# Output projection of a two-layer decoder step, issued in stages over all eight output tiles

## Chip, cores and metric

The kernel runs on one core of a Trainium2 chip. TensorE (PE) multiplies, VectorE (DVE) and ScalarE (ACT) work on its results, GpSimd (POOL) does small side work, SyncE (SP) issues all DMA transfers in one queue, in program order. The metric is the device time of one execution in microseconds, lower is better.

## What is computed

Two layers, each a SwiGLU feed-forward, a token mixer and a second feed-forward. 512 prompt tokens and 8 sample tokens (each with a state of its own) go through together. Of the mixer, this matters here:

```python
p_conv, p_z, p_b, p_a, p_q, p_k, p_v = jnp.split(h @ w_in, SPLIT_POINTS, axis=-1)
dn_out, S_new, conv_new = _deltanet(p_conv, p_z, p_b, p_a, conv_buf, S0, ...)   # 4 heads, 512 columns
swa_out = _swa_banded(q, k, v, swa_sinks)       # prompt: window of 128, 8 heads, 512 columns
swa_out, k_new, v_new = _swa_step(q, k, v, k_buf, v_buf, swa_sinks)   # samples
mix = jnp.concatenate([dn_out, swa_out], axis=-1) @ w_out     # 1024 x 1024
x = x + m[:, 5] * mix
```

The delta rule runs over chunks of the prompt, one after the other through a state S; each needs the inverse of a triangular matrix. For the samples it is one step from a state S0 of 8 x 4 matrices of 128 x 128, which is written back.

## The kernel before

Activations lie transposed (features on partitions): 8 blocks k of 128 input features, and two halves of the tokens, half 0 with 256 and half 1 with 264 columns (256 prompt, 8 samples). Weights are streamed from HBM as `raw` tiles and split by ACT and DVE into a high and a low part (`whi`/`wlo`, or `khi`/`klo` where the split block is kept in a slot of its own), each for 4 blocks k; the activations are split too (`hh`, `hl`). A product is three matmuls for each block k (`mmk`, line 659): hi x hi, hi x lo, lo x hi.

Everything is recorded in one Python pass, and each engine runs its own instructions in that order. `Clock` keeps an estimate of when each engine is free, and `Fill` holds generators of small work (delta-rule inverse, merges of the blocks of the inverse, scan, window attention, sample heads), ordered by the numbers in `RANK`. `fill.step()` puts steps of that work between the large matmuls where the estimate says that they are ready; `fill.until(cond)` records such work alone until a condition holds. So the order is set by these calls, by the ranks and by the estimates.

In `mix` (line 1036) the input projection ends with the tiles z0 to z2. What is then left is small work: for head pair 0 and 1 `dn_inverse` (a chain of 21 small operations on DVE, tiles `bb`, `w`, `t`, `wt`), `dn_merge` (tiles `XT`, `X`, `mb`, `wt`), `scan` (four chunks, tiles `kd`, `R`, `vn`, `S`), `normed` (writes `hh`/`hl`, blocks 0 to 3), `swa_chain` (window attention, blocks 4 to 7), and for the samples `dn_sample`, which does one head pair after the other in `sample_pair`: it loads the states (`s<-in_s`), multiplies them by zero-padded vectors (32 small matmuls, `aux<-s,pad`), sends a row through memory and back (`vnd`, `bv`), updates and writes the states (`s<-bv,misc,s`, `out_ss`). Only after both pairs does it write the sample columns of blocks 0 to 3 in half 1 (`hh<-on`, `hl<-on`).

The output projection is a `tail` (line 770): for half 0, output tile m = 0 to 7, each over all k; then half 1 in the same way. Its function `wait` holds half 0 until all blocks of chunks 0 and 1 are there, and half 1 until those of chunks 2 and 3 and of the samples are. `KEEP = 1` tile's weights are kept for half 1, tiles 4 to 7 stay in the ring of 8 split blocks, tiles 1 to 3 are loaded and split again. Half 0 accumulates in tiles `acc` (two of two banks each, a bank for each output tile), half 1 in `aux` (four of one bank). `xupdate` (line 689) adds a finished tile to the residual x on DVE, `Norm` sums the squares for the next norm.

Of the kernel before, what the change touches and what calls it, by code (L numbers as in the profile page):

```python
# [17 lines left out]
KD = D // 128  # L18
# [7 lines left out]
SLOTS = 51  # L26
PARTS = ((0, 11), (11, 22))
FIRST = 4
KEEP = 1
RANK = {"scan": 1.2, "merge": 9.9, "inverse": 5.4, "taps": 3.5, "front": 3, "normed": 1.0, "prep": 4.3, "keep": 7.0, "dn_s": 2.3, "swa_s": 2.0, "swa": 5.2}  # L30
BACKLOG = {"act": 2.4, "dve": 7.7}
TUNE = {"spare": 5, "steps": 8}
# [270 lines left out]
class Ops:  # L303
# [17 lines left out]
    def dma(self, out, in_):  # L321
        self.nc.sync.dma_start(out=out, in_=in_)
        nbytes = 4 * out.shape[0] * self.cols(out)
        self.clk.run("dma", max(0.45, nbytes / 330e3), [out], [in_], 1.4 if nbytes < 65536 else 2.6)

    def mm(self, out, lhsT, rhs, start, stop, frac=1.0, join=False):

        self.nc.tensor.matmul(out, lhsT=lhsT, rhs=rhs, start=start, stop=stop, skip_group_check=join)  # L328
        n = self.cols(rhs)
        if rhs.dtype == F32R:  # L330
            cost = max(0.107, n / 2400)
        else:
            cost = n / 600 if n >= 128 else 0.0033 * out.shape[0]
        cost = cost * frac + 0.011 * min(frac, 1.0)
        self.clk.run("pe", cost, [out], [lhsT, rhs])
# [43 lines left out]
    def tt(self, **k):  # L379
        self._dve("tensor_tensor", self.cols(k["out"]), k)  # L380

    def stt(self, **k):
        self._dve("scalar_tensor_tensor", self.cols(k["out"]), k)
# [22 lines left out]
def trunk(ctx, tc, xT, cT, cst, rope, vec, gu1, dn1, win, wba, wout, gu2, dn2, ada,  # L406
# [13 lines left out]
    fill = Fill(clk)  # L420

    used, given = set(), [0]

    def slot(name, dt=F32, shape=(128, NT), own=False):
        t = slot_p.tile(list(shape), dt, tag="s", name=name, bufs=SLOTS)
        if not own:
            used.add(t.tensor.name)
        return t
# [11 lines left out]
    W = Stream(ops, raw_p, hl_p, 4, 8, lambda: slot("sum", F32, (128, 512)), drop)  # L440

    def room_for(n):
        return len(used) + given[0] + n <= SLOTS - spare[0]
# [3 lines left out]
    def hold(n):  # L447

        yield lambda: room_for(n)
        given[0] += n  # L450

    def acc():
        t = ps.tile([128, 2, 512], F32, tag="acc", name="acc", bufs=2)
        clk.ring("acc", 2, t)
        return t

    def aux(shape=(128, 512)):
        t = ps.tile(list(shape), F32, tag="aux", name="aux", bufs=4)
        clk.ring("aux", 4, t)
        return t  # L460

    def small(name, shape, dt=F32, bufs=1):
        return con.tile(list(shape), dt, name=name, tag=name, bufs=bufs)
# [195 lines left out]
    def mmk(out, w, k, src, kk, a, first, last, M=128, join=False):  # L659

        wh, wl = w
        for wi, (wt_, part) in enumerate(((wh, 0), (wh, 1), (wl, 0))):
            mm(out, lhsT=wt_[:, k * M:(k + 1) * M], rhs=src(a, part, kk), start=first and wi == 0, stop=last and wi == 2,
               join=join)
# [24 lines left out]
    def xupdate(l, j, m, p, a):  # L689
        o = HALF[a][0]  # L690
        assert (l, 3 * j + 2) in mod_done
        g = mt[l][:, (3 * j + 2) * 8 + m, :]
        stt(out=x[:, m, o:o + 256], in0=p[:, 0:256], scalar=g[:, 0:1], in1=x[:, m, o:o + 256],
            op0=ALU.mult, op1=ALU.add)
        if a == 1:
            t8 = small("t8", (128, NS), bufs=2)
            tt(out=t8, in0=p[:, 256:264], in1=g[:, 1:9], op=ALU.mult)
            tt(out=x[:, m, T:NT], in0=x[:, m, T:NT], in1=t8, op=ALU.add)
# [71 lines left out]
    def tail(l, j, items, nk, norm, src, last, wait=None):  # L770

        live, ws = {}, {}
        left = [sum(it[0] == a for it in items) for a in range(2)]
        for i, (a, m, fresh, more, ring) in enumerate(items):
            o, n = HALF[a]
            if wait and (i == 0 or items[i - 1][0] != a):
                wait(a)
            if a == 0:  # L780
                if i % 2 == 0:
                    ac = acc()
                p = ac[:, i % 2, 0:n]
            else:
                p = aux()[:, 0:n]
            if fresh:
                ws[m] = []
                if ring:
                    live[m] = W.out
            for k in range(nk):  # L790
                if fresh and k % 4 == 0:
                    ws[m].append(W.take(W.out - min(live.values(), default=W.out)))
                mmk(p, ws[m][k // 4], k % 4, src, k, a, k == 0, k == nk - 1)
                if ring and not more and (k % 4 == 3 or k == nk - 1):
                    live[m] += 1
                    if k == nk - 1:
                        del live[m]
                    W.advance(min(live.values(), default=W.out))
                if k % 2:
                    fill.step()  # L800
            xupdate(l, j, m, p, a)
            left[a] -= 1
            if norm is not None:
                norm.square(m, a, left[a] == 0)
            if last:
                dma(out=y_o[:, m, o:o + n], in_=x[:, m, o:o + n])
            if norm is not None and left[a] == 0:
                norm.start(a)
# [227 lines left out]
    def mix(l, norm):  # L1036
# [269 lines left out]
        ready = set()  # L1306
# [488 lines left out]
        fill.add(dn_sample(), RANK["dn_s"])  # L1795


        kept = []

        def open_keep():  # L1800
            yield from hold(4 * KEEP)
            for _ in range(2 * KEEP):
                keeps[l].left += 1
                kept.append(1)
                W.advance(W.out)
                yield ()

        fill.add(open_keep(), RANK["keep"])
        nrm = Norm(l, 2)

        def wait(a):
            want = {(n, pr) for n in (2 * a, 2 * a + 1) for pr in range(2)} | {(n, "a") for n in (2 * a, 2 * a + 1)}
            if a:
                want |= {"s", "as"}
            fill.until(lambda: want <= ready and (a or kept))

        items = [(0, m, True, not KEEP <= m < 4, m >= KEEP) for m in range(KD)]
        items += [(1, m, KEEP <= m < 4, False, m >= KEEP) for m in (4, 5, 6, 7, *range(KEEP), *range(KEEP, 4))]
        tail(l, 1, items, KD, nrm, h_src, False, wait)
        return nrm  # L1820


# [8 lines left out]
    keeps = [Keep() for _ in range(L)]  # L1831
    def ffn_weights(gu, dn, plain=3):
        for i in range(4):
            W.add(gu[i])
        for f0, f1 in PARTS:
            for f in range(max(f0, 2), f1):
                if f < plain:
                    W.add(gu[2 * f])
                    W.add(gu[2 * f + 1])
                else:  # L1840
                    W.add_pair(gu[2 * f], gu[2 * f + 1])
            for m in range(KD):
                for c0, c1 in ((f0, f0 + 8), (f0 + 8, f1)):
                    W.add(dn[m][:, c0 * 128:c1 * 128])

    for l in range(L):
        ffn_weights(gu1[l], dn1[l], 3 if l else FIRST)
        for i in range(22):
            W.add(win[l, i])
        for m in (*range(KD), *range(KEEP, 4)):  # L1850
            W.add(wout[l, m], keeps[l] if m < KEEP else None)
        ffn_weights(gu2[l], dn2[l], 3)


    with tc.manual_schedule():
# [8 lines left out]
        def load(q, j):  # L1864

            g, c = 2 * j + q // 2, 256 * (q % 2)
            t = []
            for k in range(0, KD, 2):
                t.append(slot("ada", F32, (128, 2, 256)))
                dma(out=t[-1], in_=ada[0, g, k:k + 2, :, c:c + 256].rearrange("k p c -> p k c"))  # L1870
            return t
# [19 lines left out]
        first = [[load(0, 0), load(0, 1)]]  # L1891
# [36 lines left out]
        for l in range(L):  # L1928
            room[0] = True
            fill.add(ada_gen(l), 9)  # L1930
            opening = None if l else lambda n: first_head(n, ada_late)
            norm = ffn(l, 0, norm, lambda l=l: Norm(l, 1), False, opening, 3 if l else FIRST)
            norm = mix(l, norm)
            room[0] = True
            fill.add(ada_gen(l + 1), 9)
            nxt = (lambda l=l: Norm(l + 1, 0)) if l + 1 < L else None
            norm = ffn(l, 2, norm, nxt, l == L - 1, None, 3)
# [142 lines left out]
```

## Time and profile before

| | |
|---|---|
| median of three runs (lowest, highest) | 2230.0 us (2226.77, 2231.2) |
| the profiled execution, its time | 2231.2 us |
| its span from first to last instruction | 2229.4 us |
| PE busy, mean granted TensorE clock | 96% of the span, 0.984 |
| DVE, ACT, POOL busy | 69%, 49%, 4% |
| DMA moved | 287.76 MB, mean 129 GB/s |

The profile shows one execution. "Busy" for PE counts a matmul from start to its modelled end, also at a lowered clock, so 96% is not 96% of the highest rate. The mixer comes twice, its end at about 627 to 765 us and again 1100 us later.

### The profile page before, as it was taken

How to read it: one execution, taken by the hardware profiler on the slowest of the kernel's cores; microseconds unless marked ns; L12 is line 12 of the kernel's file. 1: busy time of each engine (PE TensorE's matmuls, PEld its weight loads, DVE VectorE, ACT ScalarE, POOL GpSimd, SP SyncE). 2: the span in 40 equal slices, each digit the busy share in tenths (PEclk: the TensorE clock that was granted, in tenths of full speed). 3: DMA queues.
4: the chain of work that ended last, by engine and by line, in shares of the span. 5: the costliest groups of instructions: out<-in, count | busy, mean ns of one | idle time of the engine just before them, and what ended most of it. 6: DMA issues, size and time to landing. Idle time of an engine off the chain costs nothing.

```text
span 2229.4 us, 43763 instructions
## 1 busy us (share of the span) xinstructions
PE 2134.5 (96%) x17254; PEld 2015.0 (90%) x17254; DVE 1541.4 (69%) x3530; ACT 1091.0 (49%) x2342; POOL 80.5 (4%) x139
## 2 busy tenths in 40 slices
PE   7999999999978999999998999999999889999999
PEld 5898899998877889889998999999988779999999
DVE  5783596567767778458748947855686678865972
ACT  4462365356744445336535634644656345542651
POOL 0000000001011000000000000000010110000000
PEclk9999999999989999999999999999999899999999
DMA  8539634343223574773322332334332242333332
GB/s 287 198 123 305 225 105 145 105 89 103 68 70 105 192 249 139 272 261 107 103 95 69 106 106 91 105 98 106 94 102 64 71 137 86 98 104 93 107 108 72
DMA packets 177534, 287.76 MB, mean 129 GB/s; under 512 B 50448, under 2 KB 96176, under 8 KB 177328
## 3 DMA queue, kind: packets, MB, share of 16 engines
q1 hardware_dynamic: 177328, 284.96, 40.7%
q8 instruction: 135, 2.21, 0.4%
q14 instruction: 71, 0.58, 0.1%
HBM read 271.55 MB, written 14.41 MB: 128 GB/s over the span
## 4 chain that ended last, share of the span: by engine, by line
PE 83%; DVE 12%; ACT 3%; issue 1%; DMA 1%; SPq 0%; DVEq 0%; ACTq 0%
PE acc L328 48%; PE aux L328 34%; DVE wlo L363 2%; PE aux L338 1%; DVE s L363 1%; DVE cy L363 1%; DVE t L363 1%; DVE hl L363 1%; DVE y L363 1%; DVE sum L363 0%; DVE x L363 0%; ACT whi L355 0%; DVE w L363 0%; ACT s L355 0%; DMA bv<-vnd 0%
## 5 line engine op out<-in xcount | busy, mean ns | idle before, releaser
L355 ACT ACTIVATE whi<-raw 128x512 fp32r<-128x512 f32 (+1 forms) x597 | 361.5, 616 | 423.3 <-PE acc L328 359.7
L328 PE MATMUL acc<-hh,whi 128*128 128x256 f32 (+1 forms) x1640 | 421.6, 294 | 18.0 <-DVE x L363 9.2
L363 DVE TENSOR_TENSOR wlo<-raw,whi 128x512 fp32r<-128x512 f32 (+1 forms) x597 | 390.6, 672 | 47.5 <-ACT whi L355 46.5
L328 PE MATMUL acc<-hh,wlo 128*128 128x256 f32 (+1 forms) x1640 | 407.0, 285 | 12.0 <-DVE wlo L363 12.0
L328 PE MATMUL acc<-hl,whi 128*128 128x256 f32 (+1 forms) x1640 | 406.8, 285 | 1.6 <-DVE hl L363 1.4
L328 PE MATMUL aux<-th,whi 128*128 128x264 f32 (+1 forms) x1800 | 338.4, 285 | 2.5 <-ACT u L355 2.4
L328 PEld LDWEIGHTS acc<-hh,whi 128*128 128x128 f32 x1640 | 288.7, 191 | 42.7 <-issue 20.4
L328 PEld LDWEIGHTS acc<-hh,wlo 128*128 128x128 f32 x1640 | 288.5, 191 | 14.4 <-DVE wlo L363 14.4
L328 PEld LDWEIGHTS acc<-hl,whi 128*128 128x128 f32 x1640 | 288.2, 191 | 2.4 <-DVE hl L363 2.2
L328 PEld LDWEIGHTS aux<-th,whi 128*128 128x128 f32 x1800 | 278.5, 189 | 6.4 <-ACT u L355 2.9
L328 PE MATMUL acc<-ghi,whi 128*128 128x256 f32 (+1 forms) x1320 | 274.3, 284 | 2.7 <-DVE x L363 2.7
L328 PE MATMUL acc<-ghi,wlo 128*128 128x256 f32 (+1 forms) x1320 | 272.2, 282 | 0.0
L328 PE MATMUL acc<-glo,whi 128*128 128x256 f32 (+1 forms) x1320 | 271.8, 282 | 0.0
L328 PE MATMUL aux<-th,wlo 128*128 128x264 f32 (+1 forms) x900 | 255.4, 284 | 0.0
L363 DVE SCALAR_TENSOR_TENSOR x<-acc,mt,x 128x256 f32<-128x256 f32 x136 | 61.6, 480 | 265.2 <-PE acc L328 265.2
L355 ACT ACTIVATE whi<-sum 128x512 fp32r<-128x512 f32 x300 | 187.8, 628 | 75.6 <-PE acc L328 39.8
L328 PEld LDWEIGHTS acc<-ghi,whi 128*128 128x128 f32 x1320 | 206.9, 188 | 16.8 <-issue 16.8
L328 PEld LDWEIGHTS acc<-ghi,wlo 128*128 128x128 f32 x1320 | 207.0, 188 | 0.0
L328 PEld LDWEIGHTS acc<-glo,whi 128*128 128x128 f32 x1320 | 206.7, 188 | 0.0
L363 DVE TENSOR_TENSOR wlo<-sum,whi 128x512 fp32r<-128x512 f32 x300 | 199.8, 686 | 8.3 <-ACT whi L355 7.3
L328 PE MATMUL aux<-hh,whi 128*128 128x264 f32 x604 | 172.6, 286 | 0.0
L328 PE MATMUL aux<-hl,whi 128*128 128x264 f32 x604 | 171.9, 285 | 0.5 <-DVE hl L363 0.5
(326 smaller groups left out, 3628.8 us busy)
## 6 DMA issues: line engine op xcount, KB each, us to landing
raw<-in_gu SPq DMA_DIRECT2D x176, 512.0 KB, 3.6
ada<-in_ada SPq DMA_DIRECT2D x288, 256.0 KB, 5.6
raw<-in_dn SPq DMA_DIRECT2D x64, 512.0 KB, 3.6
raw<-in_win SPq DMA_DIRECT2D x44, 512.0 KB, 3.8
raw<-in_dn SPq DMA_DIRECT2D x64, 192.0 KB, 3.2
raw<-in_wout SPq DMA_DIRECT2D x22, 512.0 KB, 4.5
s<-in_s SPq DMA_DIRECT2D x16, 256.0 KB, 3.9
bv<-vnd SPq DMA_DIRECT2D x16, 256.0 KB, 3.9
```

The costliest lines, as they stand in the source:

```text
L328: self.nc.tensor.matmul(out, lhsT=lhsT, rhs=rhs, start=start, stop=stop, skip_group_check=join)
L338: self.nc.tensor.transpose(out, in_, ident)
L355: self.nc.scalar.activation(**k)
L363: getattr(self.nc.vector, f)(**k)
```

## The change

The output projection no longer goes tile by tile. For half 0 all eight output tiles are open at once, two in each bank of the two large `acc` tiles. First come blocks k = 4 to 7 (window attention) for all eight tiles as soon as those of chunks 0 and 1 are there, then k = 0, 1 (first head pair) for all, then k = 2, 3 (second pair). Half 1 goes tile by tile as before, k = 4 to 7 first; between these and k = 0 to 3 of the first tile it waits for the delta rule's chunks 2 and 3 and for the samples (`"s"`). Weights come as half tiles of 128 x 512: k = 4 to 7 for half 0, eight blocks through `KEEP = 4` kept pairs of slots, k = 0 to 3 once, in the ring for both halves, and k = 4 to 7 again for half 1. That is 24 loads of 256 KB and 24 splits for each layer, where 11 loads of 512 KB and 22 splits stood.

```diff
-KEEP = 1
+KEEP = 4
@@ mix
         def open_keep():
-            yield from hold(4 * KEEP)
-            for _ in range(2 * KEEP):
-                keeps[l].left += 1
-                kept.append(1)
+            for _ in range(KEEP):
+                yield from hold(2)
+                keep.left += 1
                 W.advance(W.out)
-                yield ()
-        def wait(a):
-            want = {(n, pr) for n in (2 * a, 2 * a + 1) for pr in range(2)} | {(n, "a") for n in (2 * a, 2 * a + 1)}
-            if a:
-                want |= {"s", "as"}
-            fill.until(lambda: want <= ready and (a or kept))
-        items = [(0, m, True, not KEEP <= m < 4, m >= KEEP) for m in range(KD)]
-        items += [(1, m, KEEP <= m < 4, False, m >= KEEP) for m in (4, 5, 6, 7, *range(KEEP), *range(KEEP, 4))]
-        tail(l, 1, items, KD, nrm, h_src, False, wait)
+        units = [acc(), acc()]
+        def some(m, p, w, ks, k0, n, a, first, last):
+            for k in ks:
+                mmk(p[:, 0:n], w, k - k0, h_src, k, a, first and k == ks[0], last and k == ks[-1], join=True)
+                if k % 2:
+                    fill.step()
+        def part(m):
+            return units[m // 4][:, m // 2 % 2, 256 * (m % 2):256 * (m % 2) + 256]
+        wait((0, "a"), (1, "a"))
+        for m in range(KD):
+            w = W.take()
+            some(m, part(m), w, (4, 5, 6, 7), 4, 256, 0, m % 2 == 0, False)
+            kept(w)
+        wait((0, 0), (1, 0))
+        for m in range(KD):
+            ys.append(W.take(m))
+            some(m, part(m), ys[m], (0, 1), 0, 256, 0, False, False)
+        wait((0, 1), (1, 1))
+        for m in range(KD):
+            some(m, part(m), ys[m], (2, 3), 0, 256, 0, False, True)
+            xupdate(l, 1, m, part(m), 0)
+            nrm.square(m, 0, m == KD - 1)
+        nrm.start(0)
+        wait((2, "a"), (3, "a"), "as")
+        for m in range(KD):
+            p = aux()
+            w = W.take(W.out - y0[0])
+            some(m, p, w, (4, 5, 6, 7), 4, 264, 1, True, False)
+            kept(w)
+            if m == 0:
+                wait((2, 0), (3, 0), (2, 1), (3, 1), "s")
+            some(m, p, ys[m], (0, 1, 2, 3), 0, 264, 1, False, True)
+            xupdate(l, 1, m, p[:, 0:264], 1)
+            nrm.square(m, 1, m == KD - 1)
+        nrm.start(1)
@@ weights
-        for m in (*range(KD), *range(KEEP, 4)):
-            W.add(wout[l, m], keeps[l] if m < KEEP else None)
+        for m in range(KD):
+            W.add(wout[l, m][:, 512:1024], keeps[l])
+        for m in range(KD):
+            W.add(wout[l, m][:, 0:512])
+        for m in range(KD):
+            W.add(wout[l, m][:, 512:1024], keeps[l])
```

With this the recorded order changes around the projection. Three places follow, all in layer 0.

On DVE, the end of `dn_inverse` of the second head pair (`bb`, `w`, `wt` are its tiles) and what stands behind it; the lines with + are the changed kernel's, those with - the one's before:

```order
 L363 TENSOR_TENSOR hl_75<-so,hh_74 128x4x128 x2
-L363 TENSOR_TENSOR klo<-raw,khi 128x512 x2
-L363 TENSOR_TENSOR wlo<-raw,whi 128x512 x5
+L363 TENSOR_TENSOR klo<-raw,khi 128x512
 L363 TENSOR_TENSOR XT<-XT,aux 128x512
 L363 TENSOR_TENSOR X<-X,aux 128x512
```

```order
 L363 TENSOR_REDUCE w<-t 64x8x8
 L363 COPY wt<-w 64x256
+L363 TENSOR_TENSOR klo<-raw,khi 128x512
+L363 TENSOR_TENSOR X<-X,aux 128x512
 L363 TENSOR_TENSOR XT<-XT,aux 128x512
 L363 TENSOR_TENSOR X<-X,aux 128x512
```

Seven splits stood ahead of the inverse; now the first one does, and the second (`klo` of output tile 1, whose matmuls follow on PE as the 15th of the projection) stands right behind its last operation.

On PE, what stands ahead of the first sample pair's matmuls (`cs,vp` and then `s,pad`), first before:

```order
L328 MATMUL aux<-sq,cs 128x256
L328 MATMUL aux<-swa_5807,swa_6453 128x256 x2
L328 MATMUL aux<-swa_5807,swa_6565 128x256 x2
L328 MATMUL aux<-XT,mb 128x128 x4
L328 MATMUL aux<-X,wt_8283 128x128 x4
L338 MATMUL aux<-cs,vp 64x128
```

and with the change (`acc<-hh,whi` and the two behind it end the pass over k = 0, 1; `vn` to `QK` is a step of the second pair's scan):

```order
L328 MATMUL acc<-hh_74,whi 128x256
L328 MATMUL acc<-hl_75,whi 128x256
L328 MATMUL acc<-hh_74,wlo 128x256
L328 MATMUL aux<-swa_5807,swa_5799 128x256 x2
L328 MATMUL aux<-swa_5807,swa_5803 128x256 x2
L328 MATMUL aux<-vn,kd 128x128 x2
L328 MATMUL aux<-cy,S 128x128
L328 MATMUL aux<-QK,vn 128x128
L328 MATMUL aux<-cy,S 128x128
L328 MATMUL aux<-QK,vn 128x128
L338 MATMUL aux<-cs,vp 64x128
```

144 matmuls of the projection (k = 4 to 7 and k = 0, 1 of half 0) and the first two chunks of the second scan now stand ahead of the first sample pair; before, none of the projection did. Between the first and the second pair stand 36 projection matmuls, between the second pair and half 1's first matmul with `whi` 24.

On DVE, the end of the sample chain (`s<-bv,misc,s` are the state updates, `hh_76<-on` and `hl_77<-on` what half 1's blocks 0 to 3 wait for), first before:

```order
L363 SCALAR_TENSOR_TENSOR s_8544<-bv,misc,s_8544 128x128 x4
L363 SCALAR_TENSOR_TENSOR x<-acc,mt_80,x 128x256
L363 TENSOR_TENSOR ss<-ss,sq 128x256
L363 SCALAR_TENSOR_TENSOR s_8545<-bv,misc,s_8545 128x128 x4
L363 CAST hh_76<-on 128x4x8
L363 TENSOR_TENSOR hl_77<-on,hh_76 128x4x8
L363 SCALAR_TENSOR_TENSOR x<-acc,mt_80,x 128x256
```

and with the change (`ht`, `hl_75` are half 0's next norm):

```order
L363 SCALAR_TENSOR_TENSOR ht<-x,mt_80,rs 128x256
L363 SCALAR_TENSOR_TENSOR hl_75<-ht,mt_80,hh_74 128x256 x2
L363 SCALAR_TENSOR_TENSOR s_8802<-bv,misc,s_8802 128x128 x4
L363 SCALAR_TENSOR_TENSOR s_8803<-bv,misc,s_8803 128x128 x4
L363 CAST hh_76<-on 128x4x8
L363 TENSOR_TENSOR hl_77<-on,hh_76 128x4x8
L363 SCALAR_TENSOR_TENSOR x<-aux,mt_80,x 128x256
```

Before, half 0's last two updates of x stand behind `hh_76<-on`; now all of half 0, its next norm included, stands ahead of it.

## Rows read from the trace of the kernel before

**Rows 1.** The page: span, busy time of PE.

```profile
span 2229.4 us, 43763 instructions
PE 2134.5 (96%) x17254; PEld 2015.0 (90%) x17254; DVE 1541.4 (69%) x3530; ACT 1091.0 (49%) x2342; POOL 80.5 (4%) x139
```

**Rows 2.** Busy time in stretches: start to end, length, then as the first row says.

```profile
core 0: us, PE busy (x) PEld busy (x) DVE busy (x) ACT busy (x) POOL busy (x), PEclk, DMA share, GB/s
627.50:655.00 27.50, 17.55 (x102) 16.20 (x101) 17.16 (x42) 9.26 (x21) 5.19 (x4) 0.76 0.36 101
640.00:655.00 15.00, 10.52 (x44) 9.74 (x45) 6.70 (x12) 2.51 (x6) 5.19 (x4) 0.56 0.33 79
655.00:682.60 27.60, 26.68 (x213) 24.23 (x211) 20.39 (x65) 11.68 (x29) 3.86 (x5) 0.99 0.14 44
1727.00:1754.50 27.50, 17.52 (x101) 16.16 (x101) 17.19 (x42) 9.05 (x20) 5.19 (x4) 0.75 0.35 101
```

**Rows 3.** Timeline of PE: start, length, tiles, idle before; landmarks of the projection.

```profile
682.61 3.69 PE L328 MATMUL aux<-s,pad 128*32 128x128 f32 x64
...
704.99 0.37 PE L328 MATMUL acc<-hh,khi 128*128 128x256 f32 x1
...
715.02 3.69 PE L328 MATMUL aux<-s,pad 128*32 128x128 f32 x64
...
741.53 0.29 PE L328 MATMUL aux<-hh,whi 128*128 128x264 f32 x1
...
765.23 0.28 PE L328 MATMUL acc<-hh,whi 128*128 128x256 f32 x1
```

**Rows 4.** Timeline of DVE: end of the sample chain, then half 0's norm.

```profile
734.83 1.14 DVE L363 SCALAR_TENSOR_TENSOR s<-bv,misc,s 128x128 f32<-128x128 f32 x4 [2.68 <-DMA bv<-vnd]
...
737.66 0.18 DVE L363 CAST hh<-on 128x32 fp32r<-128x32 f32 x1
737.87 0.19 DVE L363 TENSOR_TENSOR hl<-on,hh 128x32 fp32r<-128x32 f32 x1
...
745.31 0.88 DVE L363 SCALAR_TENSOR_TENSOR ht<-x,mt,rs 128x256 f32<-128x256 f32 x2 [1.49 <-ACT rs L355]
```

**Rows 5.** The chain that ended last: start, length, what.

```profile
687.87 3.92 ACT s L355 x16
...
730.87 3.87 DMA bv<-vnd
```

**Rows 6.** Timeline of PE from 627 us.

```profile
627.49 1.16 PE L328 MATMUL aux<-XT,mb 128*128 128x128 f32 x8
628.48 1.06 PE L328 MATMUL aux<-wt,X 128*128 128x128 f32 x8
...
643.28 2.05 PE L328 MATMUL aux<-XT,mb 128*128 128x128 f32 x8 [5.30 <-DVE XT L363]
```

**Rows 7.** Timeline of DVE at the inverse.

```profile
630.21 3.09 DVE L363 TENSOR_TENSOR wlo<-raw,whi 128x512 fp32r<-128x512 f32 x5
...
634.41 0.28 DVE L363 TENSOR_SCALAR bb<-bb 64x256 f32<-64x256 f32 x1
...
642.17 0.37 DVE L363 COPY wt<-w 64x256 f32<-64x256 f32 x1
```

**Rows 8.** Timeline of PE: the next wait, and where full speed is back.

```profile
775.74 0.58 PE L328 MATMUL acc<-hh,wlo 128*128 128x256 f32 x1 [2.96 <-DVE wlo L363]
776.12 0.41 PE L328 MATMUL acc<-hh,whi 128*128 128x256 f32 x1
...
781.67 0.31 PE L328 MATMUL acc<-hh,wlo 128*128 128x256 f32 x1
```

**Rows 9.** Timeline of PE: two steps of the scan.

```profile
663.46 0.61 PE L328 MATMUL aux<-S,cy 128*128 128x128 f32 x4
663.90 1.06 PE L328 MATMUL aux<-wt,X 128*128 128x128 f32 x8
```

**Rows 10.** Waits of PE from 600 to 790 us: total, times, longest.

```profile
PE acc L328 <- DVE x L363: 4.7, 4, 1.6
```

More of the change, by code (lines that the diff above doesn't have):

```diff
@@ L1795, in mix @@
         fill.add(dn_sample(), RANK["dn_s"])
-        kept = []
+        keep = keeps[l]
         def open_keep():
-            yield from hold(4 * KEEP)
-            for _ in range(2 * KEEP):
-                keeps[l].left += 1
-                kept.append(1)
+            for _ in range(KEEP):
+                yield from hold(2)
+                keep.left += 1
                 W.advance(W.out)
-                yield ()
         fill.add(open_keep(), RANK["keep"])
         nrm = Norm(l, 2)
-        def wait(a):
-            want = {(n, pr) for n in (2 * a, 2 * a + 1) for pr in range(2)} | {(n, "a") for n in (2 * a, 2 * a + 1)}
-            if a:
-                want |= {"s", "as"}
-            fill.until(lambda: want <= ready and (a or kept))
@@ L1817, in mix, with wait @@
-        items = [(0, m, True, not KEEP <= m < 4, m >= KEEP) for m in range(KD)]
-        items += [(1, m, KEEP <= m < 4, False, m >= KEEP) for m in (4, 5, 6, 7, *range(KEEP), *range(KEEP, 4))]
-        tail(l, 1, items, KD, nrm, h_src, False, wait)
+        units = [acc(), acc()]
+        y0 = [0]
+        def wait(*want):
+            fill.until(lambda: set(want) <= ready)
+        def some(m, p, w, ks, k0, n, a, first, last):
[3 more added lines that the diff above has]
+                    fill.step()
@@ new lines, in kept @@
+        def kept(w):
+            keep.left += 1
+            W.advance(W.out if not y0[0] else y0[0])
+        def part(m):
+            return units[m // 4][:, m // 2 % 2, 256 * (m % 2):256 * (m % 2) + 256]
+        wait((0, "a"), (1, "a"))
+        fill.until(lambda: len(W.todo) > W.out or keep.left > 0)
+        for m in range(KD):
+            w = W.take()
+            some(m, part(m), w, (4, 5, 6, 7), 4, 256, 0, m % 2 == 0, False)
+            kept(w)
+        y0[0] = W.out
+        wait((0, 0), (1, 0))
@@ new lines, in mix @@
+        ys = []
+        for m in range(KD):
[16 more added lines that the diff above has]
+            some(m, p, ys[m], (0, 1, 2, 3), 0, 264, 1, False, True)
+            y0[0] += 1
+            W.advance(y0[0])
+            xupdate(l, 1, m, p[:, 0:264], 1)
+            nrm.square(m, 1, m == KD - 1)
@@ L1820, in mix @@
+        nrm.start(1)
+        given[0] = 0
         return nrm
```

## The prediction

> **What bounds the kernel now.** I read the page first. PE is busy 96% of a span of 2229.4 us [rows 1]; the profiled execution took 2231.2 us, so 1.8 us lie outside the span, and the three timed runs have a median of 2230.0, 1.2 us lower. A change that leaves PE's work as it is can only move PE's idle time and the time at a lowered clock. The projection has the same 384 matmuls of 256 or 264 columns in a layer before and after (8 tiles x 8 k x 3 x 2 halves), so I looked for idle time around it, in stretches.
>
> Between 627.5 us (the input projection is done, small work alone is left) and 655 us PE is busy 17.55 of 27.5 us, and the granted clock is 0.76; from 640 on it is 0.56, so nearly all of the 10.52 us that PE is busy there ran at the lower of the two levels. From 655 on PE is full again [rows 2]. Waste in this stretch: 9.95 us idle and half of 10.52, 5.3 us, together **15.3 us**. Layer 1 shows the same 1100 us later (17.52 us, 0.75 [rows 2]), so everything below counts twice.
>
> The landmarks on PE tell what the rest waits for [rows 3]. The samples' first head pair runs its matmuls at 682.61, the second at 715.02, the projection starts at 704.99, half 1 at 741.53, and at 765.23 the next sub-layer's first matmul ends the stage. Half 1 takes 765.23 - 741.53 = 23.7 us for 192 matmuls, 0.12 us each with the norm's one between. Half 1 needs `hh<-on`/`hl<-on`, which end at 737.87 + 0.19 = 738.06 [rows 4]: only 3.5 us before half 1 starts. From the first pair's matmuls to there it is 738.06 - 682.61 = **55.4 us**, a chain through two rounds of loads, small vector work and memory and back; the chain that ended last runs over it too (the wait for `bv`, 3.87 us, and the window attention's exponentials, 3.92 us, which stand ahead of it on ACT [rows 5]). So before, half 0 of the projection is the work that covers this chain, and it covers it with 3.5 us to spare.
>
> **The change, step by step, for one layer.**
>
> *More work ahead of the chain.* In the changed order 144 projection matmuls stand ahead of the first sample pair, 17.3 us at 0.12. So do the first steps of the second scan: 16 matmuls of 128 columns at 0.22 (the step from 663.46 to 663.90 holds two [rows 9]) and 4 transposes at half of that, 4.0 us; four matmuls of window attention go behind it, at the same rate about 1 us. If nothing of this fell into idle time, the chain would start 20.3 us later, at 702.9.
>
> *What falls into idle time.* The 15.3 us of waste at 627.5 to 655 are what the early matmuls could fill. They hardly do. At 627.49 the changed PE has 1.8 us of merge work (two groups of 0.9 [rows 6]) and 14 projection matmuls, 1.7 us, and is done at 631.0. The 15th needs the second `klo`, and that stands on DVE behind the whole inverse. Behind PE's waiting matmul then stand the merges of the first head pair, and behind them the scan. The inverse starts at 634.41 before; six splits of 0.6 us that stood ahead of it are gone (five take 3.09 [rows 7]), a split of activations (0.6) and four small operations that stood inside it (0.5 together, an estimate) move ahead: 634.4 - 3.7 + 1.1 = 631.8. It took 642.17 + 0.37 - 634.41 = 8.1 us [rows 7], 7.6 without those four; with the split of 0.7 PE goes on at 640.1, after 9.1 us idle. Before it went on at 643.28 after the 5.30 us wait, with waits before that [rows 6]. After a wait the clock falls: after 2.96 us it stayed at the lower level from 775.74 to 781.67, 6.0 us of matmuls 0.21 apart [rows 8]. At 0.12 the 28 matmuls of it would take 3.3, so 2.7 us are lost there; before, with sparser work, 5.3. I add 1.5 us for the next kept splits, which stand behind X and XT on DVE. Waste after: 9.1 + 2.7 + 1.5 = 13.3, so **2.0 us** are filled. The bounds are 0 and all of it, 15.3; I take 2.0, since the order on DVE decides it. The chain starts at 702.9 - 2.0 = 700.9.
>
> *The chain itself.* It takes 55.4 us before. The exponentials (3.92) stand behind the samples' operations on ACT now: -3.9. Half 0's next norm stands between its last updates, eleven vector operations of 0.4 (two take 0.88 [rows 4]), 4.4 us, of which 2.7 fall into the wait for `bv` that was there [rows 4]: +1.7. So 53.2 us. The bounds are 48.8 (the `bv` wait stays filled at no cost, 55.4 - 3.9 - 2.7) and 57.1 (55.4 + 1.7). While it runs, PE has only what is left: the third pass of half 0 and one block of half 1 (60 matmuls, 7.2 us), two times 3.7 us of sample matmuls, the last two steps of the scans and one block of window attention. Well under 53 us: PE will wait for loads of the second pair, and again for `hh<-on`.
>
> *The end.* `hl<-on` is done at 700.9 + 53.2 = 754.1. Then 180 matmuls of half 1 remain (the first tile's k = 4 to 7 are done), 21.8 us, and after a long wait the clock costs 2.7 us as above (bounds 0 and 5.3). The stage ends at 754.1 + 0.1 + 21.8 + 2.7 = 778.7, before 765.2: **13.5 us later**, 27 us for both layers.
>
> *The rest at nothing.* Two splits more on ACT and DVE, about 0.6 us each [rows 7], lie beside 34 us of idle ACT and 17 of idle DVE in the 55 us from 627.5 to 682.6 [rows 2]. 24 loads of 256 KB move 0.5 MB more than 11 of 512 KB, into a DMA share of 0.14 [rows 2]. The loads of the states now stand behind the weights' in SP's queue, and the last weight load ahead of them waits for a split that stands three operations behind the state S on DVE, 1.5 us; PE has the second scan's step to do meanwhile; without that cover it would be 1.5 us on the chain. With them at nothing the sum is 2231.2 + 27 = 2258; the median stands 1.2 lower: **2257 us**.
>
> **A rule against the layout of the banks.** Before, PE waits four times for updates of x, 4.7 us in all, because an `acc` tile is still being read [rows 10]. In the third pass four blocks in a row write one `acc` tile, each behind an update of the one before: six such waits, at 4.7/4 = 1.2 us about 7 us. I set them at nothing, since they lie in time in which PE waits for the chain anyhow. The Trainium skill (Perfetto Trace Analysis, section Matmuls) says that independent groups should rotate through different PSUM banks, so that the evacuation of one overlaps the next; here two groups share a bank and four a tile. If the waits were all on the path, the sum would be 14 us higher.
>
> **Rivals.**
>
> *The fill works, and it gets faster.* If the second split came early enough, all 15.3 us would be filled: the chain starts at 687.6, and with its lower bound `hl<-on` is done at 736.4; 0.1 + 21.8 + 2.7 later, at 761.0, the stage ends, 4.2 us early: 2231.2 - 8.4 - 1.2, about 2222. It decides from `hl<-on` at 740.6 on; each us there is 2 us of the whole. For it speaks the idle time of rows 2; against it the split's place behind the inverse. The Trainium skill (Perfetto Trace Analysis, section Optimization Strategy) says that interleaving regimes with different limits may improve performance; that is this rival, and the trace agrees that there is idle time to fill, not that it can be reached.
>
> *It cancels.* All of the waste filled and the chain at 53.2: `hl<-on` at 740.8, no change. So also if half is filled and the chain loses some further wait.
>
> *Worse than the sum.* Nothing filled (702.9), the chain at 57.1 and half of the six waits for x ahead of the second pair's matmuls (3.5): `hl<-on` at 763.5, the clock at its upper bound: 763.6 + 21.8 + 5.3 = 790.7, 25.5 us late, 2281. The updates of x stand among `s<-bv` on DVE, which speaks for it; that PE has time speaks against it.
>
> **How the numbers follow.** The measurement of this kernel tells 0.2%, 4.5 us, from no change. The sum, between about 2236 and 2272: 0.68. Worse: 0.15. Cancelled: 0.08. Faster: 0.09. So faster 0.09, same 0.08, slower 0.83. To leave out no more than 2 in 10, the range begins at 2231, in the middle of the cancelled case, and ends at 2279, near the worse one. The sum's own range, 2236 to 2272, stands beside it.
>
> **What would show it.** Right: PE idle for 8 to 10 us from about 631, ended by `klo`; the first `s,pad` at 697 to 704 instead of 682.6; then two waits on PE, one of some us ahead of the second `s,pad` (a load), one of over 10 us ahead of half 1's first `hh,whi`, ended by DVE's `hl<-on`; a fall of the clock behind each; the next sub-layer's first matmul at 774 to 783. Wrong: the first `s,pad` before 690; or `hl<-on` less than 48 us behind it; or no wait on it at all.

## The result, and the profile after

The changed kernel takes 2260.1 us (median of 4 runs, 2258.95 to 2261.74), the one before 2228.4 in the same comparison: ratio 1.0146, 95% interval [1.0131, 1.0161], slower. The forecast was 2257 us.

The page and the stretches of the changed kernel that answer to [rows 1, 2] (same columns):

```profile
span 2258.3 us, 43833 instructions
PE 2133.3 (94%) x17254; PEld 2015.3 (89%) x17254; DVE 1547.7 (69%) x3534; ACT 1094.3 (48%) x2346; POOL 80.0 (4%) x139
```

```profile
core 0: us, PE busy (x) PEld busy (x) DVE busy (x) ACT busy (x) POOL busy (x), PEclk, DMA share, GB/s
627.50:655.00 27.50, 16.30 (x120) 15.39 (x119) 15.54 (x36) 7.78 (x17) 5.13 (x4) 0.81 0.33 91
740.00:760.00 20.00, 8.34 (x37) 7.59 (x38) 15.00 (x46) 7.47 (x18) 0.73 (x9) 0.61 0.42 119
```

PE's busy time is nearly the same (2133.3 us, before 2134.5); its idle time grew. The gap at 627.5 was hardly filled (16.30 us busy for 120 matmuls, before 17.55 for 102, part of them at the lower clock), and a new one opened at 740 to 760, with 11.66 us idle.

PE's timeline of the changed kernel, the landmarks of [rows 3] and the waits between them (start, length, tiles, idle before and what ended it):

```profile
631.49 0.28 PE L328 MATMUL acc<-hl,khi 128*128 128x256 f32 x1
641.82 0.58 PE L328 MATMUL acc<-hh,klo 128*128 128x256 f32 x1 [10.05 <-DVE klo L363]
...
645.83 0.37 PE L328 MATMUL acc<-hh,khi 128*128 128x256 f32 x1
...
699.21 3.69 PE L328 MATMUL aux<-s,pad 128*32 128x128 f32 x64
...
715.49 0.39 PE L328 MATMUL acc<-hh,whi 128*128 128x256 f32 x1 [2.57 <-DVE x L363]
721.37 0.58 PE L328 MATMUL acc<-hh,whi 128*128 128x256 f32 x1 [3.57 <-DVE x L363]
...
733.52 3.69 PE L328 MATMUL aux<-s,pad 128*32 128x128 f32 x64
...
756.38 0.59 PE L328 MATMUL aux<-hh,whi 128*128 128x264 f32 x1 [11.31 <-DVE hh L363]
...
761.61 0.28 PE L328 MATMUL aux<-hh,klo 128*128 128x264 f32 x1
...
780.74 0.28 PE L328 MATMUL acc<-hh,whi 128*128 128x256 f32 x1
```

The first sample pair comes 16.6 us later than before (682.61), the second 18.5 us (715.02), the stage ends 15.5 us later (765.23). Layer 1 repeats it: the first pair at 1812.05 and the second at 1846.32, the stage's end at 1893.46 (before 1781.81, 1814.18 and 1864.28; layer 0's loss is in these too), the wait on `hh` again 11.30 us. So layer 1 lost 13.7 us of the 29.2 at its end. Behind the wait at 756.38 the matmuls stand 0.22 us apart up to 761.61, then 0.12: the lower of the two clock levels again.

DVE's timeline at the inverse and at the end of the sample chain, which answers to [rows 4, 7]:

```profile
633.34 0.27 DVE L363 TENSOR_SCALAR bb<-bb 64x256 f32<-64x256 f32 x1
...
640.80 0.37 DVE L363 COPY wt<-w 64x256 f32<-64x256 f32 x1
641.09 0.68 DVE L363 TENSOR_TENSOR klo<-raw,khi 128x512 fp32r<-128x512 f32 x1
...
747.98 1.13 DVE L363 SCALAR_TENSOR_TENSOR s<-bv,misc,s 128x128 f32<-128x128 f32 x4
749.03 0.48 DVE L363 SCALAR_TENSOR_TENSOR hl<-ht,mt,hh 128x256 fp32r<-128x256 f32 x1
...
753.65 0.48 DVE L363 SCALAR_TENSOR_TENSOR hl<-ht,mt,hh 128x256 fp32r<-128x256 f32 x1 [0.18 <-ACT hh L355]
754.06 2.18 DVE L363 SCALAR_TENSOR_TENSOR s<-bv,misc,s 128x128 f32<-128x128 f32 x8
756.16 0.17 DVE L363 CAST hh<-on 128x32 fp32r<-128x32 f32 x1
756.36 0.19 DVE L363 TENSOR_TENSOR hl<-on,hh 128x32 fp32r<-128x32 f32 x1
```

The second `klo` stands right behind the inverse's last `wt`. At the end, half 0's norm (`ht`, `hl`) fills DVE from 749 to 754 ahead of the last two state updates.

Waits of PE from 600 to 800 us (total, times, longest), which answer to [rows 10]:

```profile
PE aux L328 <- DVE hh L363: 11.3, 1, 11.3
PE acc L328 <- DVE klo L363: 11.2, 2, 10.1
PE acc L328 <- DVE x L363: 9.7, 4, 3.6
PE acc L328 <- DVE wlo L363: 4.4, 2, 2.7
```

Three waits are new or larger than before: on the samples, on `klo` and on x (before 4.7); the one on `wlo` is not. The experiments take them one by one, then together.

### The profile page after: what moved, and what is told of

It reads as the page before. It is cut to its first block, busy times and chain, and to the rows that moved or that the text cites. A ratio compares the mean times of both kernels' runs of the same rounds, so it can differ in the third digit from the quotient of the medians.

```text
span 2258.3 us, 43833 instructions
## 1 busy us (share of the span) xinstructions
PE 2133.3 (94%) x17254; PEld 2015.3 (89%) x17254; DVE 1547.7 (69%) x3534; ACT 1094.3 (48%) x2346; POOL 80.0 (4%) x139
## 4 chain that ended last, share of the span: by engine, by line
PE 82%; DVE 12%; ACT 2%; issue 1%; DMA 1%; SPq 0%; DVEq 0%; ACTq 0%
PE acc L328 48%; PE aux L328 34%; DVE wlo L363 2%; DVE s L363 1%; PE aux L338 1%; DVE hl L363 1%; DVE cy L363 1%; DVE t L363 1%; DVE ht L363 1%; DVE y L363 1%; DVE sum L363 0%; DMA raw<-in_wout 0%; ACT hh L355 0%; DVE w L363 0%; DVE x L363 0%
## 5 line engine op out<-in xcount | busy, mean ns | idle before, releaser
L355 ACT ACTIVATE whi<-raw 128x512 fp32r<-128x512 f32 (+1 forms) x573 | 347.9, 617 | 427.3 <-PE acc L328 351.4
L328 PE MATMUL acc<-hh,whi 128*128 128x256 f32 (+1 forms) x1592 | 409.8, 295 | 28.2 <-DVE x L363 19.4
L363 DVE TENSOR_TENSOR wlo<-raw,whi 128x512 fp32r<-128x512 f32 (+1 forms) x573 | 375.0, 671 | 50.6 <-ACT whi L355 50.0
L328 PE MATMUL acc<-hh,wlo 128*128 128x256 f32 (+1 forms) x1592 | 394.0, 285 | 11.5 <-DVE wlo L363 11.5
L328 PE MATMUL acc<-hl,whi 128*128 128x256 f32 (+1 forms) x1592 | 393.9, 285 | 1.9 <-DVE hl L363 1.8
L328 PEld LDWEIGHTS acc<-hh,whi 128*128 128x128 f32 x1592 | 279.8, 191 | 53.9 <-DVE x L363 21.0
L328 PEld LDWEIGHTS acc<-hh,wlo 128*128 128x128 f32 x1592 | 279.3, 191 | 14.0 <-DVE wlo L363 14.0
L328 PEld LDWEIGHTS acc<-hl,whi 128*128 128x128 f32 x1592 | 279.1, 191 | 3.2 <-DVE hl L363 2.9
L328 PE MATMUL aux<-hh,whi 128*128 128x264 f32 x556 | 160.1, 288 | 22.6 <-DVE hh L363 22.6
L328 PEld LDWEIGHTS aux<-th,wlo 128*128 128x128 f32 x900 | 169.3, 188 | 0.0
```

Of the source, the lines that this page charges most:

```text
L355: self.nc.scalar.activation(**k)
L363: getattr(self.nc.vector, f)(**k)
```

## The experiments

**The first pair first.**

```diff
+        wait(("pair", 0))          # added to `ready` where the pair's s,pad are recorded (that line is left out here)
         wait((0, "a"), (1, "a"))
```

> The changed kernel, but the first pass of the projection is held until the first sample pair's small matmuls are recorded, so none of the 144 matmuls stands ahead of them. Theory A (the prediction: the sample chain starts later by the work put ahead of it, and too little work is left to cover it): the first s,pad comes at 681 to 686 instead of 699.2 us, all of half 0 covers the chain again, PE's wait for hh<-on is under 3 us instead of 11.3, the stage ends at 764 to 770 us instead of 780.7, and the whole takes 2226 to 2238 us. Theory B (the tile-wide waits for the updates of x in the third pass decide, 9.7 us a layer): they stay, so the gain is under 10 us a layer and the whole is 2245 us or more.

Measured: 2258.9 us, ratio 1.0138 [1.0121, 1.0155]. PE in layer 0:

```profile
681.31 3.69 PE L328 MATMUL aux<-s,pad 128*32 128x128 f32 x64
...
728.88 3.69 PE L328 MATMUL aux<-s,pad 128*32 128x128 f32 x64
...
757.32 0.59 PE L328 MATMUL aux<-hh,whi 128*128 128x264 f32 x1 [9.56 <-DVE hh L363]
```

The first pair is back at its old place, and nothing is gained. Theory A's time did not come; 2258.9 lies in what theory B allowed (2245 or more), but B's reason, the waits for x, was not tested here. The projection's matmuls now stand ahead of the second pair (156 by the recorded order; before 42), which comes 47.6 us behind the first, so the work was only moved from ahead of the first pair to ahead of the second. And the 4.6 us that the second pair gained (733.52 to 728.88) went at the end: from there to the end of `hl<-on` it takes 28.6 us, in the changed kernel 23.0, since on DVE half 0's whole norm now stands ahead of the last updates:

```profile
755.64 0.48 DVE L363 SCALAR_TENSOR_TENSOR hl<-ht,mt,hh 128x256 fp32r<-128x256 f32 x1 [0.18 <-ACT hh L355]
756.04 1.13 DVE L363 SCALAR_TENSOR_TENSOR s<-bv,misc,s 128x128 f32<-128x128 f32 x4
```

**The low parts on GpSimd**, so that `klo` is out of DVE's queue.

```diff
-            self.ops.tt(out=lo, in0=src, in1=hi, op=ALU.subtract)
+            (pool_tt if self.subs[j][4] else self.ops.tt)(out=lo, in0=src, in1=hi, op=ALU.subtract)
```

`pool_tt` stands here for the same operation on GpSimd, `self.subs[j][4]` says that the split is a kept one.

> The changed kernel, with the low parts of the kept weights (klo) made on GpSimd instead of DVE, so that they no longer stand behind the inverse; the rest as it is. It tests the rival that the early matmuls fill PE's idle time. If the stall behind klo is all that is wrong (the rival), PE's waits for klo fall from 11.2 to under 3 us, the first s,pad comes at about 688 us and the whole takes 2222 to 2232 us. If the prediction's chain is right, the stall goes and s,pad comes 8 to 10 us earlier (689 to 692), but the chain from there keeps its 57 us and the stage ends at 770 to 773: about 2242 us, still slower than before. If something else is late at that place (the inverse's results, a load), s,pad moves by under 4 us and the whole stays at 2252 to 2262 us.

Measured: 2273.8 us, 1.0206 [1.0190, 1.0221]: slower still, outside all three forecasts, though the third was right on the place: the `klo` waits fell to 2.6 us, but others came, and the first `s,pad` came only 3.9 us earlier (695.34). The longest of the new ones, on PE:

```profile
652.11 0.58 PE L328 MATMUL acc<-hh,khi 128*128 128x256 f32 x1 [4.74 <-ACT khi L355]
```

What that `khi` waits for is a weight load, and the load stands in SP's queue right behind the eight transfers of the inverse's result (`xs<-w` to `X<-xs`, from 642.27 on); behind the weights stand the first pair's states:

```profile
651.42 0.63 ACT L355 ACTIVATE khi<-raw 128x512 fp32r<-128x512 f32 x1 [5.68 <-DMA raw<-in_wout]
...
646.42 39.34 SPq L322 DMA_DIRECT2D raw<-in_wout  x17
...
689.82 3.43 SPq L322 DMA_DIRECT2D s<-in_s  x4
```

So the fill was held by the inverse on two queues, DVE's and SP's, and this edit freed only the first. The inverse itself took longer here, 11.0 us (631.69 to 642.65) instead of 7.8: its operation `t<-w,bb` of 64x8, for one, took 0.94 us beside an operation of GpSimd (0.16 in the changed kernel) and ended with it. At the end the whole norm of half 0 (DVE, 754.3 to 761.3) stands ahead of the last state updates, and `hh<-on` comes at 764.31.

**Half 1 without the samples.** The sample columns of blocks 0 to 3 come from `zs`; the delta rule's output for the samples is left out of the projection.

```diff
         wait((0, 1), (1, 1))
+        out_sample(zs, 0)
...
-            out_sample(on, 0)
             ready.add("s")
```

> The changed kernel, but the sample columns of half 1's blocks 0 to 3 are taken from the gate tile zs ahead of the third pass: the delta rule's output for the samples is left out of the projection (all of its work, states included, is still done). This prices the wait for hh<-on. Theory A: the wait of 11.3 us and the low clock behind it (2 to 3 us) go, the stage ends at 766 to 769 instead of 780.7 us, the whole takes 2230 to 2236 us. Rival: another wait takes its place at once (second pair's transposes, loads, the residual's updates): under 5 us a layer are gained, 2250 us or more.

Measured: 2239.6 us, 1.0052 [1.0037, 1.0067], between the two forecasts; the stage ends at 771.65. So the wait on the samples with its low clock is worth 20.6 us of the 31.8 lost. About 6 us a layer remain without it; `klo` (11.2) and x (9.4) still wait there.

**The third pass alternating between the tiles.**

```diff
-        for m in range(KD):
+        for m in (0, 4, 1, 5, 2, 6, 3, 7):
             some(m, part(m), ys[m], (2, 3), 0, 256, 0, False, True)
```

> The changed kernel, with the third pass in the order m = 0, 4, 1, 5, 2, 6, 3, 7, so that neighbouring blocks write different acc tiles. Prediction's step (these waits lie in time in which PE waits for the chain anyhow): PE's waits for x fall from 9.7 to under 5 us, the wait for hh<-on grows by nearly as much, the whole takes 2254 to 2261 us. Theory B (they are on the path, since they delay the second sample pair): the second s,pad comes 5 to 7 us earlier than 733.5 and so does the stage's end, the whole takes 2245 to 2250 us.

Measured: 2266.7 us, 1.0173 [1.0158, 1.0189]: 6.5 us slower than the changed kernel, against both theories, though the waits for x fell to 5.0 us and the second `s,pad` came 0.9 us earlier (732.63). DVE shows why:

```profile
737.93 2.07 DVE L363 SCALAR_TENSOR_TENSOR ht<-x,mt,rs 128x256 f32<-128x256 f32 x2 [3.90 <-ACT rs L355]
...
740.72 0.34 DVE L363 SCALAR_TENSOR_TENSOR vr<-aux,r,vr 64x128 f32<-64x128 f32 x1
...
748.20 0.28 DVE L363 TENSOR_SCALAR vr<-vr,r 64x128 f32<-64x128 f32 x1
...
760.81 0.18 DVE L363 CAST hh<-on 128x32 fp32r<-128x32 f32 x1
```

With the third pass done sooner, the norm is recorded sooner, and the second pair's small operations (`vr`) stand behind and between its `ht`/`hl`, first behind a wait of 3.90 us for ACT's `rs`. From the second `s,pad` to the end of `hl<-on` it takes 28.6 us, in the changed kernel 23.0. This gave theory C: the place of the norm in DVE's queue.

**The norm of half 0 later.**

```diff
-        nrm.start(0)
         wait((2, "a"), (3, "a"), "as")
...
                 wait((2, 0), (3, 0), (2, 1), (3, 1), "s")
+                nrm.start(0)
```

> The changed kernel, with the next norm of half 0 started only after the wait for the samples instead of right behind the third pass; nothing else moves on TensorE but that norm's one matmul. Theory C (DVE takes its queue in order, and the norm's operations stand ahead of the last state updates and so of hh<-on): hl<-on comes 4 to 6 us earlier than 756.5, the stage ends as much earlier than 780.7, the whole takes 2248 to 2252 us. The prediction's term for it was 1.7 us a layer: 2255 to 2258 us. If the loads of bv end last there, nothing moves: 2259 to 2262 us.

Measured: 2255.4 us, 1.0118 [1.0100, 1.0136]. From the second `s,pad` to the end of `hl<-on` it takes 20.1 us (735.57 to 755.69), 2.9 less than in the changed kernel; both pairs came 1 to 2 us later; 0.7 us of that stands already at the first wait for `klo` (642.50, changed kernel 641.82), for the rest no row gives a reason. What ends last there now is a load:

```profile
752.53 1.14 DVE L363 SCALAR_TENSOR_TENSOR s<-bv,misc,s 128x128 f32<-128x128 f32 x4 [3.98 <-DMA bv<-vnd]
```

So theory C holds for a part, 2.9 us a layer on the chain; its forecast for the whole (2248 to 2252) did not come, that of the prediction's term (2255 to 2258) did. What more could be gained there is bounded by `bv`.

**Both together: alternating, norm later.**

> Both edits: the third pass in the order m = 0, 4, 1, 5, 2, 6, 3, 7 and the norm of half 0 started after the wait for the samples. The alternating order alone cost 6 us, and its norm stood ahead of the second pair's vr on DVE. Theory C: with the norm out of the way the loss is gone, and the second s,pad at about 732 us gives hl<-on at 749 to 752 and 2244 to 2250 us, up to 5 us better than the norm edit alone. If the alternating order hurts by itself (other work of DVE, TensorE's order), it stays 4 us or more behind the norm edit alone.

Measured: 2251.0 us, 1.0102 [1.0086, 1.0118], 4.5 us better than the norm edit alone. The same order that cost 6.5 us now gains, so it had cost through the norm. The waits for x were partly on the path: the second `s,pad` follows the first in 33.1 us, with the norm edit alone in 35.3.

**Both together: GpSimd, norm later.**

> Both edits: the low parts of the kept weights made on GpSimd and the norm of half 0 started after the wait for the samples. The first alone cost 13.6 us, although the first s,pad came 4 us earlier and the klo stall was gone. Theory C (its norm came to stand ahead of the second pair's updates): 2248 to 2254 us, within 3 us of the norm edit alone. If GpSimd's splits slow DVE or ACT or the early matmuls push other work back: 2260 us or more.

Measured: 2259.8 us, 1.0136 [1.0118, 1.0154]: 14 us of the loss came from the norm, but this way of filling the gap gains nothing even so (4 us slower than the norm edit alone). ACT's `khi` (6.2 us) and `vn` (4.3) are late in place of `klo`.

**Both pairs ahead, norm later.**

```diff
+        wait(("pair", 0))
         wait((0, "a"), (1, "a"))
...
+        wait(("pair", 1))
         wait((0, 0), (1, 0))          # ahead of the second pass
```

> The changed kernel, with the first pass held until the first sample pair's matmuls are recorded, the second pass held until the second pair's are, and the norm of half 0 started after the wait for the samples. Holding the first pair alone left the time at 2258.9, since the same 144 matmuls then stood ahead of the second pair (681.3 and 728.9 us, 47.6 us apart instead of 32.4). Theory A+C (what counts is TensorE's work ahead of either pair, and the norm on DVE): the first s,pad at 680 to 685, the second at 713 to 718, hl<-on at 736 to 741, the stage's end at 763 to 768 us, the whole 2224 to 2236 us. If the waits for x in the third pass are what is left (9.7 us), the stage ends at 770 or later: 2240 us or more.

Measured: 2239.5 us, 1.0050 [1.0034, 1.0066]. Two thirds of the loss are gone. The second `s,pad` is at 723.29, later than forecast; 96 matmuls stand ahead of it, and PE waited 0.3 us there for a state's load. The last of the 96 began at 704.64, though, 18.7 us earlier. What is late is DVE: the first pair's state updates begin 24.5 us behind its `s,pad` (682.98), before 14.5, behind splits of the projection's weights, one of which waits for ACT:

```profile
701.62 0.69 DVE L363 TENSOR_TENSOR klo<-raw,khi 128x512 fp32r<-128x512 f32 x1 [4.05 <-ACT khi L355]
...
707.49 2.19 DVE L363 SCALAR_TENSOR_TENSOR s<-bv,misc,s 128x128 f32<-128x128 f32 x8
```

The second pair's states are loaded only behind these updates (issued at 718.08).

**The states on another DMA queue.**

```diff
-                dma(out=st[i], in_=s0[l, :, 16 * pr + 4 * i:16 * pr + 4 * i + 4, :])
+                dma_p(out=st[i], in_=s0[l, :, 16 * pr + 4 * i:16 * pr + 4 * i + 4, :])   # nc.gpsimd; the stores too
```

> The kernel of the run before (both sample pairs ahead, norm of half 0 later: 2239.5 us), with the loads and stores of the samples' states issued from GpSimd's DMA queue instead of SP's. There five loads of weights stood ahead of the states' stores and loads in SP's queue and held it for 10.3 us; the second s,pad came 40.3 us after the first and ended a wait for the load of a state. Theory D (SP's in-order queue delays the second pair): the second s,pad comes at 715 to 719 instead of 723.3 us, the stage ends 4 to 8 us earlier than 773.7, the whole takes 2224 to 2232 us. If TensorE's 96 matmuls between the pairs set it, or issuing from GpSimd costs as much: 2236 us or more.

Measured: 2245.9 us, 1.0072 [1.0056, 1.0087]. The second `s,pad` is no earlier (724.30), so the gain of theory D did not come. That does not clear SP's queue: the move put GpSimd's own work behind the transfers. Its zeroing of `pad` for the second pair, at 697.39 in the run before, comes at 718.78, behind the stores and loads of the states, and DVE waits 4.26 us for it. The first pair's updates on DVE are as late as before this edit (24.5 us behind `s,pad`).

**As much ahead of the second pair as before.**

```diff
         for m in range(KD):
+            if m == 4:
+                wait(("pair", 1))
             w = W.take()               # first pass, the first pair ahead of it; third pass alternating, norm later
```

> The staged projection with TensorE's work ahead of the second sample pair cut to what stood there before: the first pair before the first pass, the second pair after four of its eight tiles (48 projection matmuls ahead of it; 42 before the change, 180 in the changed kernel), the third pass in the order m = 0, 4, 1, 5, 2, 6, 3, 7, the norm of half 0 after the wait for the samples. Theory A (the work put ahead of the pairs is the cause): the second s,pad at 714 to 718, hl<-on at 735 to 740, the stage's end at 762 to 767 us, the whole 2222 to 2234 us, within 0.3% of before. If the staged order costs by itself (more loads and splits, tiles held open, waits for x): 2238 us or more.

Measured: 2235.6 us, 1.0023 [1.0014, 1.0032]. The chain is nearly where it was (`hl<-on` ends at 739.02; before 738.06): the first pair's updates begin 16.5 us behind its `s,pad`. The second `s,pad` begins at 712.50, and all but its first two matmuls wait for a load until 713.76. Half 1 now begins with a wait of its own:

```profile
742.22 0.59 PE L328 MATMUL aux<-hh,klo 128*128 128x264 f32 x1 [3.81 <-DVE klo L363]
```

> The same with the states' loads and stores on GpSimd's DMA queue. Theory D: if SP's queue still delays the second pair, 2 to 8 us less than without (2218 to 2230 us). If SP's queue is no longer late there, or GpSimd's queue is slower, no change or up to 6 us more.

Measured, with the states on GpSimd's queue besides: 2244.0 us, 1.0061 [1.0049, 1.0074], 8 us worse; the second `s,pad` moves to 718.11. GpSimd's queue is the worse one here, for the reason above:

```profile
709.08 2.22 POOL L1390 DMA_DIRECT2D s<-in_s  x4
711.29 1.02 POOL L374 MEMSET pad<- 128x520 f32 x2
...
711.87 0.79 DVE L363 COPY pad<-misc 128x8 f32<-128x8 f32 x4 [2.79 <-POOL pad L374]
```

With SP's queue these zeroings began at 693.13 and 694.08. Behind the copy on DVE stands `pt`, and PE waits 3.58 us for that ahead of the second pair.

**And half 1's splits earlier.**

```diff
             some(m, part(m), ys[m], (2, 3), 0, 256, 0, False, True)
+            W.advance(y0[0])
+            W.rest()
```

`W.advance` records the next load and the high part of its split, `W.rest` the low part.

> The staged projection with both sample pairs where they stood before (the run with 48 matmuls ahead of the second pair, 2235.6 us, 3 us a layer behind the kernel before), and besides the kept splits for half 1 recorded between the blocks of the third pass instead of behind it. There half 1 began with a wait of 3.8 us for klo, which stood on DVE behind the last updates of x. If that wait is what is left of the loss: it goes, the stage ends at 764 to 766 instead of 768.3 us, and the whole takes 2227 to 2231 us, the same as before. If the three splits now delay the updates of x or hh<-on as much: 2233 to 2238 us. If what is left lies elsewhere (the wait at the inverse, 6.3 us instead of 5.3): 2232 us or more.

Measured: 2229.2 us, 0.9999 [0.9989, 1.0009]: the loss is gone. The wait for `klo` that half 1 began with is away, since its splits stand ahead of the last updates on DVE, and the stage ends within 0.3 us of where it ended before (765.23):

```profile
730.60 1.89 DVE L363 TENSOR_TENSOR klo<-raw,khi 128x512 fp32r<-128x512 f32 x3
...
739.52 0.19 DVE L363 TENSOR_TENSOR hl<-on,hh 128x32 fp32r<-128x32 f32 x1
```

```profile
765.53 0.28 PE L328 MATMUL acc<-hh,whi 128*128 128x256 f32 x1
```

Layer 0 of eight of these side by side; the first column of numbers is counted in the recorded order, the rest are starts on PE and the median:

| kernel | projection matmuls ahead of the second pair | its `s,pad` | stage's end | whole, us |
|---|---|---|---|---|
| before | 42 | 715.02 | 765.23 | 2228 to 2230 |
| splits earlier | 48 | 712.00 | 765.53 | 2229.2 |
| as much ahead as before | 48 | 712.50 | 768.34 | 2235.6 |
| both pairs ahead, norm later | 96 | 723.29 | 773.69 | 2239.5 |
| the same, other queue | 96 | 724.30 | 771.24 | 2245.9 |
| first pair first | 156 | 728.88 | 781.24 | 2258.9 |
| changed kernel | 180 | 733.52 | 780.74 | 2260.1 |
| alternating, norm later | 192 | 732.32 | 777.51 | 2251.0 |

From 48 to 180 matmuls the second pair moves by 21.5 us, 0.16 us for each, where one alone takes 0.12. That is no price of a matmul on PE: the splits on DVE and the loads that come with a pass stand ahead of the chain too, and with both pairs ahead it was those that were late.

## Why the prediction was right

**The fill: right.** Forecast was an idle PE from 631.0 to 640.1 behind the second `klo`; it was idle for 10.05 us and went on at 641.82. The lower clock lasted 4 us, not 6.0 (to 645.83). The first `s,pad` came at 699.2, forecast 700.9: of the 20.3 us of work ahead 3.7 were filled, forecast 2.0. That the gap could not be filled better even with `klo` off DVE was not forecast; the weight loads behind the inverse's transfers in SP's queue were late next.

**More work ahead of the chain: right.** The sum delayed the chain from its first pair on, and so it came, 16.6 us at the first pair. What the sum does not say: the delay does not hang on the first pair. With the first pair ahead of the work it came 18 us earlier, and nothing followed, since the same work then stood between the pairs. Only when the second pair, too, had as little ahead of it as before, the end of the chain came back (739.02 and 739.71, before 738.06). Which queue carries the delay differs: PE's in the changed kernel, DVE's with the pairs ahead.

**The chain itself: mis-sized, by 4.1 us.** Forecast 53.2 us, measured 699.21 to 756.55, 57.3, just beyond the upper bound of 57.1. Three terms made it, +3.0, +2.8 and -1.7 against the forecast:

- The exponentials ahead on ACT, forecast at -3.9: from the first `s,pad` to the first state update it took 13.65 us (to 712.86), before 14.54 (682.61 to 697.15): -0.9. DVE ran the window attention's and the scan's operations between the pair's steps instead, and the loads of `bv`, issued at 708.08 and 3.9 us to landing in the median, would have held that update until 712.0 anyhow.
- The waits for x, forecast at nothing because PE waits anyhow: they lie ahead of the second `s,pad` (715.49 and 721.37), and from the first state update to there it took 20.7 us, before 17.9: +2.8. The Trainium skill's rule against such a layout (Perfetto Trace Analysis, section Matmuls: rotate independent groups through different banks) was weighed and set aside; the runs agree with it, once the norm was out of the way: alternating brought these waits from 9.4 to 5.0 us and the whole from 2255.4 to 2251.0. Here the wait goes by the tile and not by the bank alone: output tile 2 lies in another bank than output tile 1, and its first matmul (721.37) still stood until the update of output tile 1 was done on DVE (720.84 to 721.32).
- Half 0's norm, forecast at +1.7: with it moved away the second part of the chain took 20.1 us instead of 23.0, so 2.9. Before, that part took 23.0 too, with a wait for `bv` of 2.68 [rows 4]: the norm took the place of that wait, and the part came out at 0.0 instead of +1.7.

**The end: right.** From `hl<-on` to the stage's end 24.2 us, forecast 24.6. Together: 1.7 early, 4.1 late, 0.4 early, 2.0 us, and the loss of layer 0 came out at 15.5 instead of 13.5. Layer 1's came out at 13.7. That the whole is only 3 us off the forecast is thus partly luck: the chain's terms missed by 3.0 and 2.8 us one way and by 1.7 the other, and the fill took back 1.7.

**The form of the waits: half right.** The long wait on `hh<-on` came (11.3 us), with the lower clock behind it. Ahead of the second pair a wait for a load was forecast; the waits there were for x.

**The rest at nothing: not quite.** The last run has the 24 loads and splits of the changed kernel, and with its other edits it ends where the kernel before does, so they need not cost anything. But the splits for half 1 had to be recorded early for that: recorded late, they cost about 6 us of the whole (2235.6 against 2229.2).

**The rivals.** The gain by filling did not come in either GpSimd run; but its condition was met only for `klo`, and no run brought the weight loads ahead of the inverse's transfers, so what a full fill would give stays open. Cancelling came only with the pairs held in place, the third pass alternating, the norm moved and the splits early, all together; the staged order then need not cost time. Nothing tried was faster than the kernel before.

## What to carry to other kernels

Before work is put into idle time, look for the long chain of small steps that stands behind it in the same in-order queues: what is put ahead of any of its links, the matmuls on PE or their splits on DVE, delays the end, and an earlier first link alone does not help. Look also for what the work itself waits for, on every queue; here its splits and its loads both stood behind the chain that left the engine idle. What goes behind a pass (a norm, a split) belongs in the same account on DVE: an edit that only made a pass quicker cost 6.5 us, because the norm behind it then stood ahead of the chain. Judge such an edit together with the place of what it releases.

## What the runs showed of the hardware

Issued from GpSimd's queue instead of SP's, the states' loads of 256 KB landed 3.6 us after issue in the median with both pairs ahead (on SP 4.6) and 3.9 with half of the first pass between (on SP 3.4), so not clearly later. Yet both kernels with them were slower, the first by about 5 us going by the two ratios, the second by 8.4 us. The traces show one cost: GpSimd runs its transfers and its other operations in one order, so its zeroing of `pad` moved behind them, from 697.39 to 718.78 and from 693.13 to 711.29 us, and DVE waited 4.26 and 2.79 us for it. In the first of the two, layer 0 still ended earlier (771.24, on SP 773.69); where the rest of its loss lies was not settled.

Vector operations took longer while GpSimd worked on tiles of 128x512 beside them: with `klo` on GpSimd, `t<-w,bb` of 64x8 took 0.94 us instead of 0.16 and `t<-w,bb` of 64x50 1.13 instead of 0.23, and both ended within 0.1 us of GpSimd's operation. The split itself took 1.3 us on GpSimd, 0.7 on DVE.
